# Hybrid mLSTM and attention step on one core: the output weights are gated and summed mid-kernel and kept in DRAM, the last stage leaves GpSimd, and the samples' rows lie as four column quarters

## The chip, the cores and the metric

The kernel runs on one core of one Trainium2 chip. A core has a matrix engine (TensorE, PE in the profile; its weight loads are shown apart as PEld), a vector engine (VectorE, DVE), an activation engine (ScalarE, ACT), a general engine (GpSimd, POOL) and SyncE (SP), which here only issues DMAs. The engines run side by side. Each works through its own instructions in program order, and they wait for one another by semaphores. Operands lie in SBUF (128 partitions), TensorE writes its results into banks of PSUM, and everything else lies in DRAM. In the code V, S and G stand for VectorE, ScalarE and GpSimd, `dma` for a DMA issued by SP and `mm` for a matmul.

The metric is the device time of one execution in microseconds (us), lower is better.

## The reference

One layer of a decoder is computed for 1024 prompt rows and 32 sample rows (8 sequences of 4), D = 1024, in float32:

```python
h, gate = adaln_in(x, c, w_ada, b_ada, g_norm)      # gate: one row of 1024 per sequence
(mq, mk, mv, mi, mf, mo, mz, aq, ak, av, az, gm, ga) = split_in(h @ w_in)
y_m, C, n, m = mlstm_branch(...)                     # 4 heads of 128
y_a = sliding-window attention with sinks(...)       # 8 heads of 64, window 128
u = sigmoid(gm) * (y_m @ w_mo) + sigmoid(ga) * (y_a @ w_ao)
x = x + gate * (u @ w_o)
y = rmsnorm(x, g_final)                              # rows of the prompt: y_p, of the samples: y_s
```

The mLSTM states, the kept keys and values and some smaller outputs are written as well. The last two lines matter here. All prompt rows share one gate row of 1024 values, so that `gate * (u @ w_o)` is the same as `u @ (w_o * gate)` with each column of `w_o` scaled by its gate value. The sample rows have gates of their own.

## The kernel before, in words

**Arithmetic.** TensorE multiplies in a short format (float32r in the code). A float32 operand is therefore split into a high half (a rounded copy, made by ScalarE) and a low half (the operand minus the high half, made by VectorE or GpSimd), and a product is three matmuls: high by high, high by low and low by high. Names ending in `h` and `l` (`u3whA`, `u3wlA`, `wo_t1l`) are such halves. Large products are cut into 2 by 2 blocks and formed from seven products of sums of blocks in place of eight products. The seven operands made of a weight's blocks are called `b11`, `b21`, `b22`, `t1` to `t4` here.

**Stages.** The layer norm and h (to about 66 us of the span), then the heads' projections, the attention and the mLSTM in jobs that a planner interleaves (to about 617 us), then `att_out` and `mem_out`, eight jobs each, which multiply by `w_ao` and `w_mo` and add up u (617 to 741 us), and the last stage, u @ w_o with the residual and the last norm (from 741 us).

**What sets the order.** Up to 617 us a planner (`side`, a list of generators on named streams) decides what comes next: each generator yields the modelled time until its next step may be placed, so the order on every engine comes from the planner's costs. `job` interleaves the outputs of one product with the loads and splits of the next. In the last stage the order is written out by hand: `V.on = S.on = G.on = True` keeps the instructions of each engine in the order of the program. SP issues all DMAs of this part from one queue in order, and its DMAs take turns on eight semaphores, so that a DMA cannot be issued before the one eight places ahead of it has landed.

**`mem_out`, before.** While the eight jobs run, SP loads the sixteen 128x512 pieces of `w_out`, VectorE forms the sums of blocks (`out_sums`), ScalarE and VectorE or GpSimd split the results into the high and low halves `wo_...h` and `wo_...l` that the last stage uses. For d above 5 the addition to u is on GpSimd.

**The last stage, before.** Four blocks of 256 rows (class `Rows`); each has the seven products, 6 matmuls each, and four plain products of 12 matmuls, 90 matmuls of 128x512 in all. The results lie in four PSUM banks `foX`, `foW`, `foY`, `foZ`; `copied` copies one bank to another (ScalarE), from where the next products are added to it. `Rows.start` makes the halves of a block's row operands (`u3whA` and `u3wlA` are those of block 3) while the block ahead of it runs. `add_part` multiplies a result by the gate (`gbc`) into `fot` and adds it to the residual rows in `rows_l`; `gated_ahead` does the same on GpSimd for the results `foy` and `fop`. `norm_rows` sums the squares and finds the reciprocal root by three Newton steps (`recip_sqrt`; names `fv`, `fr_w`, `fr_y`), and `rows_out` multiplies by it and by `g_final` (`gf`) and stores y_p.

**The sample rows.** `sample_rows` is a generator that the last stage advances at fixed places (`aside`). It multiplies the 32 sample rows of u by the unscaled `w_out`, which is loaded a second time: per half of 512 columns there are eight steps k, which go in turn to the four column groups of the array (32 columns each), so that four partial sums lie below one another in a bank `fo`; they are added by VectorE into `fo8s`, and GpSimd applies gate and residual.

Line numbers of the profile: L273 is the helper of all matmuls, L221 that of all VectorE, ScalarE and GpSimd operations, L260 that of SP's DMAs.

Of the kernel before, what the change touches and what calls it, by code (L numbers as in the profile page):

```python
# [174 lines left out]
def body(tc, a):  # L175
    nc = tc.nc
    with ExitStack() as ctx:
# [102 lines left out]
        def recip_sqrt(half, shape, name):  # L280
# [5 lines left out]
            for _ in range(3):  # L286
                if shape[1] == 1:
                    V.scalar_tensor_tensor(w, yi, half, yi, op0=ALU.mult, op1=ALU.mult)
                else:
                    V.tensor_tensor(w, yi, yi, op=ALU.mult)  # L290
                    V.tensor_tensor(w, w, half, op=ALU.mult)
                V.scalar_tensor_tensor(yi, w, 1.5, yi, op0=ALU.subtract, op1=ALU.mult)
# [755 lines left out]
        def head(h):  # L1048
# [100 lines left out]
            for visit in ([(load, 0), 10.0, ""], [(prep, 0), 3.0, "o"], [(stage_e, 0), (stage_a, 0), 5.0, "o"],  # L1149
# [5 lines left out]
                for fn, p in visit[:-2]:  # L1155
                    fn(p)
                yield visit[-2:]
# [7 lines left out]
        def sample_head(h):  # L1165
# [39 lines left out]
            yield 4.0, ""  # L1205
            V.tensor_tensor(et, et, S_[:NS], op=ALU.mult)
            for vf, vm, w in vms:
                S.copy(vm[0:32, :w], vf[:, :w])
            yield 2.5, ""
            for vf, vm, w in vms:  # L1210
                V.tensor_tensor(vm[32:64, :w], vf[:, :w], vm[0:32, :w].bitcast(F32), op=ALU.subtract)
# [35 lines left out]


# [104 lines left out]

        OPERANDS = {1: "b11", 2: "b21", 3: "b22", 4: "t4", 5: "t1", 6: "t2", 7: "t3"}
# [453 lines left out]
        ymx = [lambda k, c0, n, x=x: ymt[x][:, k, c0:c0 + n] for x in range(2)]  # L1808
        for d in range(KT):
# [3 lines left out]
        wo, plain, held = {n: [] for n in ("b11", "b21", "b22", "t1", "t2", "t3", "t4")}, {}, {}  # L1813

        def out_split(name, t, eng):
            wo[name].append(tuple(ht([128, 512], f"wo_{name}{x}", F32R) for x in "hl"))
            hi, lo = wo[name][-1]
            S.copy(hi, t)
            eng.tensor_tensor(lo, t, hi.bitcast(F32), op=ALU.subtract)

        def out_sums(k):

            (b11, b12), (b21, b22) = held.pop(k), held.pop(k + 2)
            out_split("b22", b22, G)
            V.tensor_tensor(b22, b22, b12, op=ALU.subtract)
            V.tensor_tensor(b12, b12, b11, op=ALU.subtract)
            out_split("t1", b12, G)
            V.tensor_tensor(b11, b11, b22, op=ALU.add)
            out_split("b21", b21, G)
            out_split("t3", b22, V)  # L1830
            V.tensor_tensor(b21, b21, b11, op=ALU.subtract)
            out_split("t2", b11, G)
            out_split("t4", b21, V)

        for d, k in enumerate((0, 2, 1, 3, 4, 5, 6, 7)):
            mem_out(d, ymx, u)
            raws = []
            for i in range(2):
                raws.append(raw_tile(f"wo{k}_{i}").rearrange("p k n -> p (k n)"))
                dma(raws[i], a["w_out"][k * 128:(k + 1) * 128, HALF[i]], True)  # L1840
            if k < 4:
                held[k] = raws
                if k < 2:
                    out_split("b11", raws[0], V)
                else:
                    out_sums(k - 2)
                continue
            for i, raw in enumerate(raws):
                plain[k, i] = (ht([128, 512], f"wo_h{k}", F32R), ht([128, 512], f"wo_l{k}", F32R) if (k, i) == (7, 1) else
                               granule(f"wo_l{k}", "wr", 9, F32R).rearrange("p k n -> p (k n)"))  # L1850
                S.copy(plain[k, i][0], raw)
                (G if i else V).tensor_tensor(plain[k, i][1], raw, plain[k, i][0].bitcast(F32), op=ALU.subtract)

# [4 lines left out]
        gbc, gsb, gf = misc[:3]  # L1858
        dma(gbc, gbD.to_broadcast((128, D)))
        dma(gf, a["g_final"].to_broadcast((128, D)))  # L1860
        dma(gsb[:NS], gsD)

        def residual(tb, n):
            xb = misc[3 + tb % 4 if tb < 8 else 7]
            dma(xb[:n], a["x_prompt"][tb * 128:tb * 128 + 128] if tb < 8 else a["x_sample"])
            return xb

        def add_part(xb, src, gb, n, cf, ss, mult=V, add=V):
            t = ht([128, 512], "fot")[:n, :cf.stop - cf.start]
            mult.tensor_tensor(t, src, gb[:n, cf], op=ALU.mult)  # L1870
            add.tensor_tensor(xb[:n, cf], xb[:n, cf], t, op=ALU.add)
            if ss is not None:
                square(xb[:n, cf], ss)

        def norm_rows(ss, m, parts):
# [6 lines left out]
            return recip_sqrt(v, [128, m], f"fr{m}")  # L1882

        def rows_out(tb, xb, r, by=V):
            yo, n = (a["y_p"][tb * 128:tb * 128 + 128], 128) if tb < 8 else (a["y_s"], NS)
            for c, eng in zip(HALF[::-1], (by, V if tb == 7 else by)):
                if eng is S:
                    S.activation(xb[:n, c], xb[:n, c], AF.Copy, scale=r[:n])
# [273 lines left out]
```

## Time and profile before

| | |
|---|---|
| time, three runs | 848.74, 850.94, 850.16 us (median 850.16) |
| profiled execution, its own time | 851.53 us |
| its span in the profile | 849.7 us |
| TensorE matmuls busy | 816.6 us (96%) |
| TensorE weight loads busy | 681.2 us (80%), under matmuls |
| VectorE busy | 614.9 us (72%) |
| ScalarE busy | 393.9 us (46%) |
| GpSimd busy | 172.9 us (20%) |
| read from DRAM, written | 110.78 MB, 41.61 MB |

All times in the views are counted from the start of the span, and the profiled execution took 1.83 us outside it. A busy share of 96% says that TensorE bounds the kernel as a whole; what is left are the stretches in which it waits, the stretches in which its clock is reduced, and what lies ahead of its first and behind its last matmul. A row of the timeline gives start, duration, engine, line, operation, output<-inputs and shape, and in square brackets the idle time before it with the instruction that ended it. Rows marked x2 or x4 hold several like instructions in a row. [...]

### The profile page before, as it was taken

The page shows a single profiled execution, that of the slowest core. Times are in us where ns is not written, and L with a number is a line of the kernel's source. Part 1 is how long each engine was busy: PE and PEld are TensorE (multiplying, and loading weights), DVE is VectorE, ACT ScalarE, POOL GpSimd, SP SyncE. Part 2 cuts the span into 40 slices and gives each one's busy share as a digit, 9 for nine tenths or more (in the row PEclk, how much of TensorE's full clock was granted, in tenths as well). Part 3 has the DMA queues.
Part 4 walks back from the last instruction along what each step waited for, and adds up shares of the span by engine and source line. Part 5 has one row for each costly group of instructions (what it writes and reads, how often), then busy time and mean ns, then how long its engine had stood idle before and what let it go on. Part 6 is the DMA issues. An engine that isn't in the chain of part 4 may idle for free. (4 is left out here: it accounts for less than half of the span.)

```text
span 849.7 us, 15293 instructions
## 1 busy us (share of the span) xinstructions
PE 816.6 (96%) x5083; PEld 681.2 (80%) x5083; DVE 614.9 (72%) x1634; ACT 393.9 (46%) x987; POOL 172.9 (20%) x236
## 2 busy tenths in 40 slices
PE   6899999999999899999999999999999999999984
PEld 3689988887899678778887777777788999967863
DVE  3787796666776867767667566888766679857987
ACT  4672356656654444455445344434443333223334
POOL 0220000330332335111211000000012033532563
PEclk9999999999999899999999999999999999999988
DMA  9996766775758866664534445553335974272322
GB/s 329 364 364 201 193 180 202 204 235 175 219 159 241 214 178 149 173 191 116 154 101 133 126 122 143 163 165 106 112 92 192 348 257 137 89 248 84 112 100 105
DMA packets 125330, 152.39 MB, mean 179 GB/s; under 512 B 28912, under 2 KB 79856, under 8 KB 125220
## 3 DMA queue, kind: packets, MB, share of 16 engines
q1 hardware_dynamic: 121028, 145.12, 55.1%
q0 software_dynamic: 4224, 6.30, 3.2%
q8 instruction: 40, 0.66, 0.3%
q14 instruction: 38, 0.31, 0.1%
HBM read 110.78 MB, written 41.61 MB: 179 GB/s over the span
## 5 line engine op out<-in xcount | busy, mean ns | idle before, releaser
L256 POOL DMA_DIRECT2D yhD<-yt x48 | 28.8, 606 | 114.3 <-DVE yt L221 108.0
L273 PE MATMUL g_w_ao<-ya,wh_w_ao 128*128 128x384 f32 (+1 forms) x192 | 45.7, 322 | 0.1
L273 PE MATMUL g_w_mo<-ym_l,wh_w_mo 128*128 128x384 f32 (+1 forms) x192 | 45.7, 323 | 0.0
L221 ACT ACTIVATE p<-p,nmx 128x256 f32<-128x256 f32 (+1 forms) x64 | 31.0, 486 | 23.2 <-DVE nmx L221 20.6
L256 POOL DMA_DIRECT2D mkN<-mkt x44 | 26.9, 618 | 50.6 <-DVE mkt L221 23.5
L273 PEld LDWEIGHTS g_w_ao<-ya,wh_w_ao 128*128 128x128 f32 x192 | 33.4, 188 | 0.7 <-DVE ya L221 0.6
L273 PEld LDWEIGHTS g_w_mo<-ym_l,wh_w_mo 128*128 128x128 f32 x192 | 33.5, 188 | 0.0
L273 PE MATMUL g_aq<-h_h,wh_aq 128*128 128x384 f32 (+1 forms) x96 | 32.5, 339 | 0.0
L256 POOL DMA_DIRECT2D mvN<-mvt x40 | 24.8, 625 | 35.5 <-DVE mvt L221 22.0
L221 DVE CUSTOM_DVE_ANT_0 p<-sc,cst,sink 128x256 f32<-128x256 f32 (+1 forms) x64 | 26.0, 461 | 7.5 <-PE sc L273 7.5
L273 PE MATMUL g_aq<-h_h,wl_aq 128*128 128x384 f32 (+1 forms) x96 | 31.0, 323 | 0.0
L273 PE MATMUL g_aq<-h_l,wh_aq 128*128 128x384 f32 (+1 forms) x96 | 31.0, 323 | 0.0
L273 PE MATMUL g_w_mo<-ym_l,wl_w_mo 128*128 128x384 f32 (+1 forms) x96 | 31.0, 323 | 0.0
L273 PE MATMUL g_w_ao<-ya,wl_w_ao 128*128 128x384 f32 (+1 forms) x96 | 30.8, 321 | 0.0
L273 PE MATMUL g_mq<-h_h,wh_mq 128*128 128x384 f32 (+1 forms) x72 | 24.9, 345 | 0.0
L273 PE MATMUL g_mk<-h_h,wh_mk 128*128 128x384 f32 (+1 forms) x72 | 24.5, 340 | 0.0
L273 PE MATMUL g_mk<-h_l,wh_mk 128*128 128x384 f32 (+1 forms) x72 | 23.3, 323 | 0.0
L273 PE MATMUL g_mq<-h_l,wh_mq 128*128 128x384 f32 (+1 forms) x72 | 23.2, 323 | 0.0
L273 PE MATMUL g_mk<-h_h,wl_mk 128*128 128x384 f32 (+1 forms) x72 | 23.2, 323 | 0.0
L221 POOL TENSOR_TENSOR ya<-yr,ya 128x384 fp32r<-128x384 f32 (+1 forms) x6 | 7.3, 1229 | 78.4 <-DVE hg L221 65.0
L273 PE MATMUL g_mq<-h_h,wl_mq 128*128 128x384 f32 (+1 forms) x72 | 23.2, 323 | 0.0
L221 POOL COPY qs<-mk 128x32 f32<-128x32 f32 x3 | 0.6, 212 | 104.6 <-ACT mk L221 104.6
(1702 smaller groups left out, 2803.0 us busy)
## 6 DMA issues: line engine op xcount, KB each, us to landing
hb<-hD SPq DMA_DIRECT2D x24, 256.0 KB
x<-xT SPq DMA_DIRECT2D x16, 256.0 KB
early_h<-w_ada SPq DMA_DIRECT2D x8, 512.0 KB
hD<-x SPq DMA_DIRECT2D x16, 256.0 KB
adar_ga<-w_ada SPq DMA_DIRECT2D x16, 256.0 KB
wr_ga<-w SPq DMA_DIRECT2D x16, 256.0 KB
wr_gm<-w SPq DMA_DIRECT2D x16, 256.0 KB
taD<-gt SPq DMA_DIRECT2D x16, 256.0 KB
```

The lines of the kernel that those rows point to most:

```text
L221: ins = f(*args, **kw)
L256: nc.gpsimd.dma_start(out, in_)
L273: in_order(nc.tensor.matmul(out, lhsT, rhs, start=start, stop=stop, skip_group_check=more))
```

## The change

1. **Scaled weights, mid-kernel.** A new generator `out_weights` is put on the planner's stream "x" in the stage of the last head. It loads the prompt's gate row (`ogb`) and `w_out` once, in four batches of four 128x512 pieces, multiplies them by the gate on VectorE (16 operations), forms the block sums there (8 operations), and stores the 14 operand tiles (`woD`) and the 8 plain tiles (`wpD`), 256 KB each, in DRAM.
2. **`att_out` and `mem_out`** load these 22 tiles (`out_load`) and split each one job later (`out_split`: high half on ScalarE, low half on VectorE). The sums and GpSimd's splits are gone from there, and all additions to u are on VectorE.
3. **The last stage** needs no multiplication by the gate: `add_part` is one addition on VectorE, and `gated_ahead` and `final_gain` are gone. GpSimd keeps only the Newton steps of the norm, 12 operations of 128x2 or 128x1 per pair of row blocks (the very last norm stays on VectorE); the squares are taken one by one, and one high half goes to y_p through ScalarE's DMA queue.
4. **The sample rows** lie as four quarters of 256 columns in four groups of 32 partitions: each step k has four matmuls of 256 columns, one for each column group, and no partial sums are left to add. The weights come 512 KB at a time, two tiles, in four loads. Residual, gate and `g_final` come by twelve small DMAs, and the sum of squares over the quarters by four small matmuls (`ft`).
5. In the sample heads of the middle, copies and splits of `vm` are spread over more planner steps.

```diff
-        def recip_sqrt(half, shape, name):
+        def recip_sqrt(half, shape, name, eng=V):
...
+                    eng.tensor_tensor(w, yi, yi, op=ALU.mult)
+                    eng.tensor_tensor(w, w, half, op=ALU.mult)
+                if eng is V:
+                    V.scalar_tensor_tensor(yi, w, 1.5, yi, op0=ALU.subtract, op1=ALU.mult)
+                else:
+                    eng.tensor_scalar(w, w, 1.5, None, op0=ALU.subtract)
+                    eng.tensor_tensor(yi, w, yi, op=ALU.mult)
...
+                if h == NH - 1 and visit[0] == (stage_b, 2):
+                    side.add("x", out_weights())
...
+        def out_weights():
+            gb = [ht([128, 512], f"ogb{i}") for i in range(2)]
...
+            def scaled(ks):
+                ts = []
+                for k in ks:
+                    for i in range(2):
+                        ts.append(ht([128, 512], f"ow{i}"))
+                        dma(ts[-1], a["w_out"][k * 128:(k + 1) * 128, HALF[i]])
+                yield 7.0, ""
+                for j, t in enumerate(ts):
+                    V.tensor_tensor(t, t, gb[j % 2], op=ALU.mult)
+                    if j % 2:
+                        yield 1.5, ""
+                return ts
+            for k in range(2):
+                b11, b12, b21, b22 = yield from scaled((k, k + 2))
+                for n, t in (("b11", b11), ("b22", b22), ("b21", b21)):
+                    store(woD[n][k], t)
+                yield 8.0, ""
+                V.tensor_tensor(b22, b22, b12, op=ALU.subtract)
+                V.tensor_tensor(b12, b12, b11, op=ALU.subtract)
+                yield 1.5, ""
...
+            for k in (4, 6):
+                ts = yield from scaled((k, k + 1))
+                for j, t in enumerate(ts):
+                    store(wpD[k - 4 + j // 2, j % 2], t)
+                yield 4.0, ""
...
-                (G if d > 5 else V).tensor_tensor(us, us, t, op=ALU.add)
+                V.tensor_tensor(us, us, t, op=ALU.add)
...
+        def out_split():
+            while coming:
+                hi, lo = coming.pop(0)
+                S.copy(hi, lo.bitcast(F32))
+                V.tensor_tensor(lo, lo.bitcast(F32), hi.bitcast(F32), op=ALU.subtract)
+        early, mid = dict(((4, 1), (5, 1), (6, 1), (7, 3))), (3, 3, 2, 2, 2, 2, 2, 0)
...
+        for d in range(KT):
             mem_out(d, ymx, u)
+            out_split()
+            out_load(mid[d])
...
-        def add_part(xb, src, gb, n, cf, ss, mult=V, add=V):
-            t = ht([128, 512], "fot")[:n, :cf.stop - cf.start]
-            mult.tensor_tensor(t, src, gb[:n, cf], op=ALU.mult)
-            add.tensor_tensor(xb[:n, cf], xb[:n, cf], t, op=ALU.add)
+        def add_part(xb, src, cf, ss=None):
+            V.tensor_tensor(xb[:, cf], src, xb[:, cf], op=ALU.add)
...
-        def norm_rows(ss, m, parts):
+        def norm_rows(ss, m, parts, eng=G):
...
+            load(0)
+            by_quarter(gs8, gsD)
+            by_quarter(x8, a["x_sample"])
+            by_quarter(gf8, a["g_final"].to_broadcast((NS, D)))
             yield
+            for k0 in (0, 2, 4, 6):
+                for k in (k0, k0 + 1):
+                    for j in range(4):
+                        mm(acc[32 * j:32 * j + 32], u(k, SEQ, NS), raws[k % 2][:, 256 * j:256 * j + 256],
+                           start=(k == 0), stop=(k == KT - 1), share=4)
+                if k0 < 6:
+                    load(k0 + 2)
                 yield
```

**How the order moves.** First VectorE in the last stage, between block 2 and block 3. Before, from the last use of `foZ` of block 2, with `u3wlB` and `u3wlC` the low halves for block 3:

```order
L221 TENSOR_TENSOR fot<-foZ,rows_l_8802 128x512
L221 SCALAR_TENSOR_TENSOR rows_l_8803<-rows_l_8803,fr_y,rows_l_8802 128x512 x4
L221 TENSOR_TENSOR u3wlB<-u_h_7748,u3whB 128x256
L221 TENSOR_TENSOR u_h_7748<-u_h_7748 128x2x128
L221 TENSOR_TENSOR u3wlB<-u_h_7748,u3whB 128x256
L221 TENSOR_TENSOR fot<-foW,rows_l_8802 128x512
L221 TENSOR_TENSOR rows_l_8802<-rows_l_8802,fot 128x512
L221 TENSOR_TENSOR u3wlC<-u_h_7749,u3whC 128x512
```

The same place in the changed kernel, with the rows ahead of it that lead up to it:

```order
L221 TENSOR_TENSOR u_h_7838<-u_h_7838 128x2x128 x2
L221 SCALAR_TENSOR_TENSOR rows_l_8875<-rows_l_8875,fr_y,rows_l_8874 128x512 x2
L221 TENSOR_TENSOR rows_l_8875<-foy_9413,rows_l_8875 128x512
L221 TENSOR_TENSOR rows_l_8875<-foZ,rows_l_8875 128x512
L221 SCALAR_TENSOR_TENSOR rows_l_8875<-rows_l_8875,fr_y,rows_l_8874 128x512 x2
L221 TENSOR_TENSOR u3wlB<-u_h_7838,u3whB 128x256
L221 TENSOR_TENSOR u_h_7838<-u_h_7838 128x2x128
L221 TENSOR_TENSOR u3wlB<-u_h_7838,u3whB 128x256
L221 TENSOR_TENSOR rows_l_8874<-foW,rows_l_8874 128x512
```

Two of the four row outputs have moved ahead of the work on `foy` and `foZ`, the multiplication into `fot` is gone, and the nine Newton operations that stood ahead of the first `fot` row before are no longer on this engine.

Next GpSimd in the last stage. Before, at the same place (`fop` and `foy` are results that wait for gate and residual, `fo8s` the sample sums):

```order
L221 TENSOR_TENSOR fop_9233<-fop_9233,rows_l_8802 128x512
L221 TENSOR_TENSOR rows_l_8802<-rows_l_8802,fop_9233 128x512
L221 TENSOR_TENSOR fot<-fo8s,rows_l_8802 32x512
L221 TENSOR_TENSOR rows_l_8803<-rows_l_8803,fot 32x512
L221 TENSOR_TENSOR foy_9325<-foy_9325,rows_l_8802 128x512
L221 TENSOR_TENSOR rows_l_8803<-rows_l_8803,foy_9325 128x512
L221 TENSOR_TENSOR rows_l_8803<-rows_l_8803,fot 128x512
```

In the changed kernel GpSimd's whole work there is made of such rows (the last three on the samples' rows, then the first on the next row block):

```order
L221 TENSOR_TENSOR fr_w<-fr_w,fv_9343 128x1
L221 TENSOR_SCALAR fr_w<-fr_w 128x1
L221 TENSOR_TENSOR fr_y<-fr_w,fr_y 128x1
L221 TENSOR_TENSOR fr_w<-fr_y 128x2
L221 TENSOR_TENSOR fr_w<-fr_w,fv 128x2
L221 TENSOR_SCALAR fr_w<-fr_w 128x2
L221 TENSOR_TENSOR fr_y<-fr_w,fr_y 128x2
```

All operations of 512 columns have left this engine, and the Newton steps have come to it from VectorE.

Last SP's queue in the middle of the kernel, where `wr_ga` and `wr_gm` are raw weights, `taD` and `tmD` stored gate halves, and `C_p` and `n_p` outputs. Before:

```order
L260 DMA wr_ga_1_5721<-w 128x512
L260 DMA C_p<-C 128x128
L260 DMA n_p<-C 128x1
L260 DMA taD_161<-gts 128x32
L260 DMA tmD_169<-gts 128x32
L260 DMA wr_gm_0_5723<-w 128x512
```

In the changed kernel, from the first store of a scaled tile:

```order
L260 DMA woD_b_157<-ow_5497 128x512
L260 DMA woD_b_158<-ow_5501 128x512
L260 DMA taD_169<-gt 128x512
L260 DMA C_p<-C 128x128
L260 DMA woD_b_159<-ow_5503 128x512
L260 DMA n_p<-C 128x1
L260 DMA wr_gm_0_5742<-w 128x512
L260 DMA wr_gm_1_5744<-w 128x512
```

The weights `wr_gm` of the next products stand behind three stores, each of which can be issued only when VectorE has scaled its tile.

More of the change, by code (lines that the diff above doesn't have):

```diff
@@ L1812, in body @@
                 split(ymD, *ymx, PCOLS, d // 2)
[L1813 to L1835, printed above, removed]
-            mem_out(d, ymx, u)
[L1837 to L1852, printed above, removed]
+            out_split()
+            out_load(early.get(d, 0))
+        for d in range(KT):
+            mem_out(d, ymx, u)
+            out_split()
+            out_load(mid[d])
+        assert not items and not coming
         assert not due
@@ new lines, in sample_rows @@
+            s8 = sm([128, 1], "fs8", 1)
+            square(x8, s8)
+            yield
+            tot = po([128, 1], "ft8")
+            for j in range(4):
+                mm(tot[32 * j:32 * j + 32], cst[:, C_S32:C_S32 + NS], s8, start=True, stop=True, share=4)
+            v8 = sm([128, 1], "fv8", 1)
+            V.tensor_scalar(v8, tot, 0.5 / D, 0.5 * EPS, op0=ALU.mult, op1=ALU.add)
+            r8 = recip_sqrt(v8, [128, 1], "fr1", G)
+            yield
+            V.scalar_tensor_tensor(x8, x8, r8, gf8, op0=ALU.mult, op1=ALU.mult)
@@ L1937, in body @@
+            for j in range(4):
+                dma(a["y_s"][:, 256 * j:256 * j + 256], x8[32 * j:32 * j + 32])
         class Rows:
```

177 lines of the change are left out of this document (86 added, 91 removed).

## The prediction

> **What bounds the kernel now.** I read the page first, then PE's waits in the last stage, a table of stretches, and the timelines at each wait. The page's busy shares:
>
> ```profile
> PE 816.6 (96%) x5083; PEld 681.2 (80%) x5083; DVE 614.9 (72%) x1634; ACT 393.9 (46%) x987; POOL 172.9 (20%) x236
> PEclk9999999999999899999999999999999999999988
> ```
>
> PE is busy nearly throughout, so only three things can be gained: waits of PE, a lowered clock (the digits 8 at the end of the second row), and what follows the last matmul. PE's waits from 740 us to its last matmul (total, times, longest):
>
> ```profile
> PE foX L273 <- ACT foW L221: 4.2, 2, 4.0
> PE fo L273 <- DMA rows_l<-w_out: 0.9, 1, 0.9
> ```
>
> The busy time of the engines by stretch (PE, PEld, DVE, ACT, POOL, granted clock, DMA share, GB/s):
>
> ```profile
> 430.00:450.00 20.00, 20.00 (x122) 16.32 (x121) 12.54 (x42) 8.05 (x19) 2.45 (x4) 1.00 0.44 120
> 540.00:560.00 20.00, 20.00 (x131) 16.07 (x131) 19.09 (x42) 10.08 (x22) 0.00 (x0) 1.00 0.52 161
> 700.00:720.00 20.00, 20.00 (x125) 20.00 (x124) 18.03 (x30) 5.38 (x10) 5.96 (x4) 1.00 0.45 136
> 786.00:810.00 24.00, 24.00 (x107) 19.84 (x107) 21.90 (x39) 8.93 (x23) 12.84 (x9) 1.00 0.32 99
> 810.00:838.00 28.00, 23.56 (x116) 19.71 (x114) 24.21 (x43) 12.70 (x32) 18.71 (x14) 0.88 0.32 113
> ```
>
> The middle and `mem_out` keep PE at 20.00 of 20, and the loss lies in the last 28 us, where the clock falls to 0.88. PE there:
>
> ```profile
> 812.13 0.39 PE L273 MATMUL foZ<-wo_t1l,u3whA 128*128 128x512 f32 x1
> 812.36 0.39 PE L273 MATMUL foZ<-wo_t1h,u3wlA 128*128 128x512 f32 x1
> 816.76 0.79 PE L273 MATMUL foX<-wo_b21h,u3whB 128*128 128x512 f32 x1 [4.02 <-ACT foW L221]
> 817.35 0.63 PE L273 MATMUL foX<-wo_b21l,u3whB 128*128 128x512 f32 x1
> 821.94 0.40 PE L273 MATMUL foX<-wo_h,u3whC 128*128 128x512 f32 x1
> ```
>
> In stream two starts lie 0.23 us apart (812.13 to 812.36; 0.2265 over longer runs). Between 812.36 and 821.94 lie thirteen steps, 2.94 us at that pace, and 9.58 went by: **6.64 us lost**, 4.17 as the wait and 2.47 as twelve slow steps of 0.43 behind it. The copy that PE waited for had itself waited for DVE:
>
> ```profile
> 816.14 0.57 ACT L221 COPY foW<-foX 128x512 f32<-128x512 f32 x1 [8.35 <-DVE fot L221]
> ```
>
> And DVE was late, because operations with two inputs in SBUF take longer beside POOL (DVE rows, then POOL's):
>
> ```profile
> 802.32 1.51 DVE L221 TENSOR_TENSOR u_h<-u_h 128x256 f32<-128x256 f32 x1
> 804.30 0.43 DVE L221 TENSOR_TENSOR u3wlA<-u_h,u3whA 128x256 fp32r<-128x256 f32 x1 [0.47 <-ACT u3whA L221]
> 806.42 1.25 DVE L221 TENSOR_SCALAR fv<-fss 128x2 f32<-128x2 f32 x1
> 809.95 0.69 DVE L221 TENSOR_TENSOR fot<-foZ,rows_l 128x512 f32<-128x512 f32 x1
> 810.56 3.76 DVE L221 SCALAR_TENSOR_TENSOR rows_l<-rows_l,fr_y,rows_l 128x512 f32<-128x512 f32 x4
> 815.37 0.68 DVE L221 TENSOR_TENSOR fot<-foW,rows_l 128x512 f32<-128x512 f32 x1
> ...
> 802.19 1.35 POOL L221 TENSOR_TENSOR rows_l<-rows_l,fot 32x512 f32<-32x512 f32 x1
> 806.29 1.35 POOL L221 TENSOR_TENSOR rows_l<-rows_l,foy 128x512 f32<-128x512 f32 x1
> ```
>
> The 128x256 operation at 802.32 took 1.51 us beside POOL, its like at 804.30 without it 0.43. `fv`, two columns wide, took 1.25 and ended at 807.67, POOL's operation at 807.64.
>
> **The change part by part.**
>
> *The stall.* Per row block DVE did nine Newton operations, four row outputs and six pairs of gate and add beside 12.84 us of POOL, 21.90 us of 24.00. Now for a block, by these rows: operand splits and sums 16 x about 0.42 (6.7), six additions at 0.69 (4.1), four row outputs at 0.75 (3.0), four small ones (0.7): an estimate of 14.5 us in a block of 90 x 0.2265 = 20.4 us. With 5.9 us to spare per block, the read of `foW` should no longer be late. Term **-6.64** (bounds: 0 if DVE still lags as much, -6.64).
>
> *The samples' wait.* Before and in a later group of eight:
>
> ```profile
> 752.84 1.06 PE L273 MATMUL fo<-rows_l,u_h 128*32 128x512 f32 x6
> 754.75 1.04 PE L273 MATMUL fo<-rows_l,u_h 128*32 128x512 f32 x2 [0.85 <-DMA rows_l<-w_out]
> 755.73 0.50 PE L273 MATMUL foZ<-wo_h,u0whD 128*128 128x512 f32 x1
> 777.58 1.06 PE L273 MATMUL fo<-rows_l,u_h 128*32 128x512 f32 x8
> 778.58 0.50 PE L273 MATMUL foZ<-wo_h,u1whD 128*128 128x512 f32 x1
> ```
>
> The first took 2.89 us, the later one 1.00. Its first products now stand at the end of block 0, some 15 us after the load can start: **-1.89**. The new groups have eight matmuls of 256 columns; I take 1.0 us each, as before (a group of half the columns can be no dearer by these rows; 0.5 each would be -2).
>
> *New waits there.* Two of the three later loads have 24 matmuls, 5.4 us, between their issue and their use. A load of 1 MB in the trace:
>
> ```profile
> 762.47 2.18 SPq L260 DMA_DIRECT2D rows_l<-w_out  x4
> 766.00:768.00 2.00, 2.00 (x11) 1.65 (x10) 1.16 (x2) 0.00 (x0) 0.00 (x0) 1.00 0.56 211
> 768.00:770.00 2.00, 2.00 (x10) 1.66 (x9) 1.90 (x4) 0.98 (x2) 0.00 (x0) 1.00 0.00 0
> ```
>
> From the first issue to empty DMA engines it is 4.6 us (by the share 0.56 of 766 to 768, about 767.1) to 5.5. Against 5.4 the wait is 0 to about 0.3, more where y_p stores or residual rows stand ahead in SP's queue. **+0.5** (0 to +2.5).
>
> *The start.* PE's second, short wait for `foW` (4.2 less 4.0, about 0.2 us) lay beside POOL's last additions to u: **-0.2** (0 to -0.7).
>
> *The tail.*
>
> ```profile
> 837.30 0.28 PE L273 MATMUL foY<-wo_h,u3wlD 128*128 128x256 f32 x1
> 835.49 1.21 DVE L221 SCALAR_TENSOR_TENSOR fr_y<-fr_w,fr_y 128x1 f32<-128x1 f32 x1
> 838.43 0.16 DVE L221 SCALAR_TENSOR_TENSOR fr_y<-fr_w,fr_y 128x1 f32<-128x1 f32 x1
> 844.95 0.75 DVE L221 SCALAR_TENSOR_TENSOR rows_l<-rows_l,fr_y,rows_l 128x512 f32<-128x512 f32 x1
> 834.15 1.29 POOL L221 TENSOR_TENSOR rows_l<-rows_l,foy 128x512 f32<-128x512 f32 x1
> 37.45 0.32 POOL L221 TENSOR_TENSOR h_l<-xS,h_h 128x64 fp32r<-128x64 f32 x1
> 36.25 0.82 POOL L221 TENSOR_TENSOR xS<-xS,B 128x64 f32<-128x64 f32 x1
> ```
>
> PE ends at 837.58, and the span 12.1 us later. Block 6's Newton steps, each held by a POOL operation, ended at 838.59, and DVE still had both remaining results to gate and add. Now POOL does these steps. They can start some 3.6 us ahead of PE's end (behind the last `foW`, its square and `fv`). Nothing of 128x1 is in the trace on POOL; the nearest are the two POOL rows of 128x64, 0.32 alone and 0.82 beside DVE. By 0.35 a step, twelve take 4.2 us and end 0.6 us after PE. Then come DVE's two row outputs (1.5), two additions (0.85), square and sums (0.75), its own Newton steps (1.7), the output (0.75) and the last store as before (4.0 from 845.7): 10.2 us after PE in place of 12.1. **-1.9** (-4 with steps of 0.2, +3.5 with 0.8, since DVE waits behind them in order). [...]
>
> *`ft`, extra small operations:* **+0.3**, four 32-column matmuls with their loads.
>
> *The middle:* 24 x 0.69 = 16.6 us more on DVE over about 110 us, where it is busy 12.5 to 14 of 20 us and 19.09 at 540, and 10 MB of DMA at a share of 0.44 to 0.52. What hides it is the lead of the splits over PE:
>
> ```profile
> 549.65 0.68 DVE L221 TENSOR_TENSOR wl_phead_gate__6690<-wr_mo,wh_phead_gate__6689 128x512 fp32r<-128x512 f32 x1
> 556.35 0.39 PE L273 MATMUL bx<-h_h,wl_phead_gate__6690 128*128 128x512 f32 x1
> ```
>
> This one, in the fullest stretch, is ready 6.0 us early. **0** (0 to +3). In `mem_out` DVE loses POOL's company and its sums and gains twelve splits and six additions, about 5.3 us per job of 7: **0**.
>
> Sum: -6.64 - 1.89 + 0.5 - 0.2 - 1.9 + 0.3 = -9.8, from 851.53 to 841.7. That execution lies 1.37 above the median of 850.16, so against the runs I expect **840.3 us**.
>
> **The rivals.**
>
> *A. DVE stays behind.* In a block DVE's row outputs wait in order for POOL's Newton chain, and behind them stand the next block's splits. As `fv` waited for POOL until 807.64, each of the twelve POOL steps may wait for a DVE operation of 0.42 to 0.75. Against it: once DVE stands still the chain runs free, so it holds DVE for at most 12 x 0.32 = 3.8 us per block, less than the 5.9 spare. If it happens all the same, or DVE's long operations weren't POOL's doing (the change then doesn't do what it says), I take half of the 6.64 to stay, in one stall of 3 to 4 us or several short ones: 840.3 + 3.3 = 843.6, up to 847 with all of it. [...]
>
> *B. The gain is eaten.* The stall goes, but POOL's chain at the end takes 0.8 a step (+5.4 against my sum) and each of three sample loads costs 1 us (+2.5): 848.2, no change. For it: no POOL operation so small is in the trace, and the 128x64 rows vary from 0.32 to 0.82. Against it: DVE has little to do while the last chain runs.
>
> *C. Slower: the middle.* SP issues in order, and stores of `woD` stand ahead of `wr_gm`. Each can be issued only when DVE has scaled its tile, and that waits for its load. If this holds SP or DVE longer than the 6.0 us lead, PE waits. A wait that lowers the clock costs 6.64, as at 812; two such would give 840.3 + 13.3 = 853.6, and slower begins from 12.4 us of waits. For C: DVE's 19.09 of 20. Against: in the stretch at 430, where the first batch falls, DVE is idle 7.5 of 20 us. [...]
>
> **How the numbers follow.** Chances: the forecast 0.58, A 0.22, B 0.09, C 0.11. The forecast's own range is 836 (tail -4, groups at 0.5 us) to 843; the whole range runs to 848, through A and up to B, and leaves out C, half of B and the best luck. What cannot be told from no change is 0.3%, 2.5 us: above 847.6 to 852.7. Forecast, A and a third of B give faster 0.83; the rest of B and a mild C give 0.08 the same; C in full gives 0.09 slower.
>
> **What would show it.** Right: no idle PE of more than 1 us behind 741 us, a granted clock of 1.00 from 810 to PE's end, DVE's 128x256 operations at 0.42 throughout, DVE's busy time near 15 us per row block. The last matmul comes some 8 us earlier, and 10 us lie behind it. Wrong: a wait of `fo8` for `w_out` above 1 us, POOL rows `fr_w` above 0.5 us with DVE idle before the row outputs, or PE idle between 430 and 740 us behind `wl_` or `wr_` tiles.

## The result and the profile after

The changed kernel takes 841.83 us (median of four runs, 840.93 to 842.38), the kernel before 849.45 us beside it: a ratio of 0.9907 (95% interval 0.9889 to 0.9926), 7.6 us less. The forecast was 840.3 us in a range of 836 to 848, so the direction and the range held, and the gain was 7.6 to 8.3 us (by the two medians of before) where 9.8 were worked out. The profiled execution took 842.23 us with a span of 840.4, to be set against 851.53 and 849.7.

The page of the changed kernel, shares of busy time and granted clock:

```profile
PE 812.5 (97%) x5123; PEld 680.3 (81%) x5123; DVE 596.4 (71%) x1636; ACT 387.4 (46%) x975; POOL 117.0 (14%) x245
PEclk9999999999999999999999999999999999999998
HBM read 116.55 MB, written 47.37 MB: 195 GB/s over the span
```

The lowered clock of the last fortieths is gone but for the tail, and 11.5 MB more are moved. PE's waits from 420 us to the end are a single row, and not behind the `wl_` or `wr_` tiles that the prediction named:

```profile
PE sU L273 <- DVE Cs L221: 1.3, 1, 1.3
```

The last stage by row block (columns as before), and PE's first and last matmul in it:

```profile
741.00:761.00 20.00, 20.00 (x105) 16.11 (x105) 9.86 (x22) 6.32 (x16) 0.00 (x0) 1.00 0.59 204
761.00:784.00 23.00, 23.00 (x131) 17.22 (x133) 11.51 (x25) 7.43 (x19) 2.71 (x12) 1.00 0.51 173
784.00:808.00 24.00, 24.00 (x121) 19.27 (x114) 15.62 (x37) 9.98 (x27) 6.50 (x24) 1.00 0.29 102
808.00:830.70 22.70, 22.63 (x123) 19.51 (x121) 10.98 (x25) 7.18 (x20) 5.26 (x24) 1.00 0.27 94
...
742.42 0.40 PE L273 MATMUL foX<-wo_h,u0whA 128*128 128x512 f32 x1
830.35 0.28 PE L273 MATMUL foY<-wo_h,u3wlD 128*128 128x256 f32 x1
```

PE is never idle there, the clock is 1.00 throughout, and DVE, which had 21.90 of 24.00 and 24.21 of 28.00 us before, has 10 to 15.6. Block 2's place, where DVE was late, now reads:

```profile
805.93 0.43 DVE L221 TENSOR_TENSOR u3wlB<-u_h,u3whB 128x256 fp32r<-128x256 f32 x1
806.39 0.43 DVE L221 TENSOR_TENSOR u_h<-u_h 128x256 f32<-128x256 f32 x1
807.07 0.68 DVE L221 TENSOR_TENSOR rows_l<-foW,rows_l 128x512 f32<-128x512 f32 x1
```

**Time by part.** With the last stage from its first matmul's start to its last one's end, and the tail from there to the end of the span, the two profiles divide like this (us):

| | before | after | difference |
|---|---|---|---|
| span up to the last stage | 740.83 | 742.42 | +1.59 |
| last stage | 96.75 | 88.21 | -8.54 |
| tail | 12.12 | 9.77 | -2.35 |
| span | 849.70 | 840.40 | -9.30 |

The same table for every kernel run here. The first column is the one that scatters: it goes from 738.98 to 746.77 over seven profiles whose code is the same up to the last stage (the changed kernel twice, e1, e5, e6, e8 and e6 with another tail order).

| kernel | to last stage | last stage | tail | median time |
|---|---|---|---|---|
| changed | 742.42 | 88.21 | 9.77 | 841.83 |
| changed, again | 738.98 | 88.21 | 9.81 | 841.17 |
| e1 GpSimd busy | 740.90 | 91.67 | 10.53 | 845.10 |
| e5 last norm on VectorE | 741.08 | 88.21 | 9.71 | 841.22 |
| e6 all norms on VectorE | 741.06 | 88.21 | 9.13 | 840.14 |
| e7 later scaling | 739.60 | 88.22 | 9.88 | 840.81 |
| e8 waits | 739.58 | 89.84 | 9.78 | 842.51 |
| e9 no scaling operations | 737.17 | 88.21 | 10.12 | 838.70 |
| e6 with another tail order | 746.77 | 88.21 | 8.22 | 840.98 |
| before, e2 less gate | 741.66 | 92.84 | 10.60 | 845.29 |
| before, e3 GpSimd silent | 739.39 | 89.44 | 8.07 | 838.17 |
| before, e4 no sample sums | 740.42 | 91.15 | 14.93 | 847.80 |
| before, e10 all on VectorE | 738.97 | 92.14 | 13.59 | 847.41 |

### The profile page after: what moved, and what is told of

Its sections match the earlier page's. It is cut to its first block, busy times and chain, and to the rows that moved or that the text cites. A ratio compares the mean times of both kernels' runs of the same rounds, so it can differ in the third digit from the quotient of the medians.

```text
span 840.4 us, 15436 instructions
## 1 busy us (share of the span) xinstructions
PE 812.5 (97%) x5123; PEld 680.3 (81%) x5123; DVE 596.4 (71%) x1636; ACT 387.4 (46%) x975; POOL 117.0 (14%) x245
## 5 line engine op out<-in xcount | busy, mean ns | idle before, releaser
L221 POOL TENSOR_TENSOR fr_w<-fr_y 128x2 f32<-128x2 f32 (+1 forms) x15 | 3.1, 208 | 159.5 <-DVE fr_y L221 139.3
L221 ACT ACTIVATE gt<-gt 128x512 f32<-128x512 f32 (+1 forms) x17 | 10.4, 613 | 25.3 <-DVE gt L221 24.7
```

The lines of the kernel that those rows point to most:

```text
L221: ins = f(*args, **kw)
```

## The experiments

The theory from the prediction (A) was that the stall of 4.02 us and the slow steps behind it came from VectorE being held up by GpSimd on top of its own load. The first rivals are that GpSimd's company alone, the gate's multiplications alone, or the samples' work in block 2 made it.

**e1: company without the work.** Nine additions on GpSimd are put into each row block:

```diff
+        def pool_busy(n):
+            for _ in range(n):
+                G.tensor_tensor(idle[1], idle[0], idle[0], op=ALU.add)
...
             add_part(xb[0], p5, hi)
+            pool_busy(3)
```

> The changed kernel with nine useless additions of 128x512 on GpSimd put back into each row block of the last stage (11 to 12 us per block, about what GpSimd did there before; nothing waits for their results). Theory A: the stall came from the lengthening of VectorE's operations beside GpSimd together with VectorE's own load, and both had to go; VectorE now needs 10 to 13 us of the 20 to 22 per block, and company adds 4 to 7, so it stays below the block's time: 128x256 operations at 0.8 to 1.5 us in place of 0.42, but PE waits under 1 us in the stage and the time rises by 0 to 2 us (842 to 844). Theory B: GpSimd's company alone makes the stall: a wait of 3 us or more of foX for ACT's copy is back with slow steps behind it, +5 to +7 us (847 to 849).

Measured: 845.1 us (ratio 0.9951, 0.9929 to 0.9973). The wait for `foW` did not come back; three smaller ones came, and the stage grew by 3.46 us:

```profile
PE ft L273 <- ACT sq L221: 1.2, 1, 1.2
PE foY L273 <- ACT foy L221: 1.1, 1, 1.1
PE foZ L273 <- DVE u0wlD L221: 0.6, 1, 0.6
```

So B is out, and A's figures (waits under 1 us, 0 to 2 us) were too low: with VectorE at 16.7 of 22 us in block 2 there is still slack on average, and PE waits all the same, since single chains (the samples' sum, the copy of `foy`) have none. Company cost 3.46 us of the stage here, where it did not fill VectorE.

**e2: the kernel before without VectorE's gate multiplications** (for `foX`, `foW`, `foY`):

```diff
-            mult.tensor_tensor(t, src, gb[:n, cf], op=ALU.mult)
-            add.tensor_tensor(xb[:n, cf], xb[:n, cf], t, op=ALU.add)
+            if mult is V and add is V:
+                V.tensor_tensor(xb[:n, cf], src, xb[:n, cf], op=ALU.add)
```

> The kernel before, with the gate's multiplication left out where VectorE did both the multiplication and the addition (the results foX, foW and foY are added ungated, so the output differs); GpSimd's work is as before. VectorE loses three operations of 0.69 us per row block. Theory A (load and company together, with samples' work in block 2): only about 0.7 to 1.4 us of what is lost stands in the 16 us of full VectorE work ahead of the late read of foW, so a wait of 2 to 3.5 us stays, and the time falls by 1 to 2.5 us (847 to 848.5). Theory C (the multiplications were the cause): the wait is gone, -6 to -7 us (843).

Measured: 845.29 us (0.9947, 0.9930 to 0.9963).

```profile
816.03 0.50 PE L273 MATMUL foX<-wo_b21h,u3whB 128*128 128x512 f32 x1 [2.24 <-ACT foW L221]
816.37 0.39 PE L273 MATMUL foX<-wo_b21l,u3whB 128*128 128x512 f32 x1
816.60 0.40 PE L273 MATMUL foX<-wo_b21h,u3wlB 128*128 128x512 f32 x1
```

The wait is 2.24 us, inside A's 2 to 3.5, and C is out. But the time fell by 4.3 us in place of 1 to 2.5: no slow steps follow the shorter wait (starts 0.23 us apart). The stage is 3.91 us shorter, as 1.8 us less of waiting took the 2.5 of slow steps with it, and the tail 1.52, which A had not counted. The last section shows that waits of about this length are followed by slow steps in some executions and not in others, so the 2.5 need not be won in each.

**e3: the kernel before with GpSimd silent** in the last stage:

```diff
-            G.tensor_tensor(t, t, gbc[:, c], op=ALU.mult)
-            G.tensor_tensor(xb[:, c], xb[:, c], t, op=ALU.add)
+            pass
```

and likewise for the final gain, the samples' gate and residual, and the addition of `foZ`.

> The kernel before, with all of GpSimd's operations of the last stage left out (its gates, residual additions and final gain, so the output differs); VectorE does what it did. Theory A: VectorE's 128x256 operations take 0.42 throughout, its small operations 0.17, the four seconds it lacked ahead of foW are there, the stall and its slow steps vanish (-6.6 us) and the tail is shorter by 2 to 3 us since its Newton steps are no longer held: 839.5 to 841.5. Theory C: VectorE's operations keep their lengths, and the stall stays within 1 us.

Measured: 838.17 us (0.9873, 0.9849 to 0.9898). PE's waits and VectorE's groups in block 2:

```profile
PE fo L273 <- DMA rows_l<-w_out: 0.2, 1, 0.2
PE foX L273 <- ACT foW L221: 0.2, 1, 0.2
...
L221 DVE SCALAR_TENSOR_TENSOR rows_l<-rows_l,fr_y,rows_l 128x512 f32<-128x512 f32 x3 | 2.2, 744 | 0.0
L221 DVE TENSOR_TENSOR u_h<-u_h 128x256 f32<-128x256 f32 x4 | 1.7, 422 | 0.1
```

VectorE still multiplies by the gate, adds the samples and takes its Newton steps. An operation on `u_h` takes 422 ns on average; the one at 802.32 took 1.51 us before. With GpSimd silent the stall is gone, and the tail is 4.05 us shorter, more than expected, which puts the time below A's range. VectorE could also have been late by waiting for results of GpSimd, but the rows exclude that: from `fot<-foX` of block 2 to `fot<-foW` it takes 16.06 us before (799.31 to 815.37) and 10.52 here (797.14 to 807.66), and its one wait for another engine in between is 0.47 us for ScalarE in both. The difference is in the length of its operations. This settles that GpSimd's operations made VectorE late.

**e4: the kernel before without the samples' sums**, six operations on VectorE and four on GpSimd:

```diff
-                for j in (32, 64, 96):
-                    V.tensor_tensor(sums[f], acc[f][j:j + 32], sums[f], op=ALU.add)
...
-            for f in range(2):
-                add_part(xb, sums[f], gsb, NS, HALF[f], None, G, G)
```

> The kernel before, with the adding up of the samples' partial sums on VectorE (six operations of 0.69) and their gate and residual on GpSimd (four operations of 32x512, 1.35 to 1.7 each) left out, so y_s is wrong. Rival D: the samples' work in block 2 was the drop too much: VectorE gains 2.1 us of its own and about 3 us of lengthening there, against a wait of 4.0: wait under 0.5 us, no slow steps, -5.5 to -6.6 us (843 to 844). Theory A without D: the stall would need the load of all the blocks, and 2 us or more of the wait stays.

Measured: 847.80 us (0.9981, 0.9968 to 0.9995). The wait shrank to 1.35 us without slow steps, between the two expectations, and the stage by 5.60 us. But the time fell only by 1.8: the tail grew from 12.12 to 14.93. The rows say why (VectorE, then GpSimd):

```profile
824.41 1.21 DVE L221 SCALAR_TENSOR_TENSOR fv<-fss,fv 128x3 f32<-128x3 f32 x1
829.07 1.21 DVE L221 SCALAR_TENSOR_TENSOR fr_y<-fr_w,fr_y 128x3 f32<-128x3 f32 x1
836.77 0.42 DVE L221 TENSOR_TENSOR fot<-foY,rows_l 128x256 f32<-128x256 f32 x1
...
819.75 5.85 POOL L221 TENSOR_TENSOR rows_l<-rows_l,rows_l 128x512 f32<-128x512 f32 x4
833.09 1.27 POOL L221 TENSOR_TENSOR rows_l<-rows_l,rows_l 128x512 f32<-128x512 f32 x1 [2.83 <-ACT sq L221]
837.74 1.26 POOL L221 TENSOR_TENSOR rows_l<-rows_l,rows_l 128x512 f32<-128x512 f32 x1 [3.37 <-ACT sq L221]
```

PE ended at 831.57, and VectorE read its last results 5.2 us later, because its small operations took up to 1.21 us, as at 835.49 before (0.16 at 838.43). The gain in the stage came off PE's end and was given back behind it. Relieving PE alone was worth little; the tail's own GpSimd work had to go too.

**e10: was the amount of work the matter?** All of GpSimd's operations of the stage go to VectorE in the kernel before (`G` becomes `V` in the places of e3):

> The kernel before, with all of GpSimd's operations of the last stage given to VectorE, the gate's multiplications kept: nothing in the middle is changed and nothing is stored in DRAM. VectorE needs 15 to 16 us per row block without GpSimd's company (measured with those operations left out), and gets 3.5 more, in block 2 another 2.8: 19 to 22 of about 22. Theory A (the company was the cause, not the amount of work): a wait of foX for foW of at most 1.5 us, no slow steps, the last matmul 5 to 7 us earlier in its stage, and 841 to 845 us. Rival B (the gate's work had to leave the stage): the wait of 3 us or more is back, and the time is within 2 us of 849.6.

Measured: 847.41 us (0.9972, 0.9952 to 0.9993).

```profile
PE foZ L273 <- DVE u0wlD L221: 1.3, 1, 1.3
PE foZ L273 <- DVE u2wlD L221: 0.8, 1, 0.8
PE foX L273 <- ACT foW L221: 0.4, 2, 0.2
```

The wait for `foW` stays away, as A has it, but neither A nor B came out whole, as the time lies between them: splits are late instead, and the tail is 13.59 us, as the additions and gains stand in one queue. So GpSimd's company had to go, and the work could not simply be moved to VectorE. That gating the weights ahead of time is what lets VectorE take the rest is argued and not shown apart: no run has the gating without the new layout of the samples' rows and the new order.

**The tail.** In the changed kernel VectorE waited for GpSimd's Newton steps from 829.08 to 830.86, across PE's end at 830.63:

```profile
828.43 0.70 POOL L221 TENSOR_TENSOR fr_w<-fr_w,fv 128x1 f32<-128x1 f32 x1
830.63 0.19 POOL L221 TENSOR_TENSOR fr_y<-fr_w,fr_y 128x1 f32<-128x1 f32 x1
828.38 0.69 DVE L221 TENSOR_TENSOR rows_l<-rows_l,rows_l 128x512 f32<-128x512 f32 x1 [0.84 <-ACT sq L221]
830.86 1.41 DVE L221 SCALAR_TENSOR_TENSOR rows_l<-rows_l,fr_y,rows_l 128x512 f32<-128x512 f32 x2 [1.78 <-POOL fr_y L221]
832.19 0.74 DVE L221 TENSOR_TENSOR rows_l<-foY,rows_l 128x256 f32<-128x256 f32 x2
```

e5 is `rs = norm_rows(ss, 1, 2, V)` in the last block:

> The changed kernel with the Newton steps of row block 6 (the norm ahead of the last one) on VectorE in place of GpSimd. In the changed kernel VectorE waited 1.78 us for GpSimd's last step behind PE's end. Theory A (order on VectorE decides): the steps take 1.4 us of VectorE ahead of the addition of foZ, and the square of that row, the gain and the two row outputs still follow one another, so that the last row is only 0.2 to 0.6 us earlier (841.3 to 841.7). Rival B: the whole wait of 1.78 us goes: 840.0.

Measured: 841.22 us (0.9906, 0.9891 to 0.9920). The last additions end 1.78 us behind PE in place of 2.30, 0.52 earlier and inside A's 0.2 to 0.6, though 1.78 us of waiting for GpSimd went: the addition of `foZ`, its square and the gain still stand one behind another. The end of the span came only 0.06 us earlier behind PE (tail 9.71 against 9.77), as the last output was followed by 4.45 us in place of 3.96. (The expectation for the last version gives 1.64 in place of the 1.78 of these rows.)

e6 has all norms on VectorE, the samples' too:

> The changed kernel with all Newton steps on VectorE, none on GpSimd. Theory A (VectorE has 7 to 10 us to spare per row block once gate and samples are gone): 1.8 us more per block do not reach PE, no wait in the stage, the same time as with the last norm alone moved (841 to 842). Rival B (moving the steps off VectorE was needed): waits of foX or of a split of 1 us or more return in blocks 2 or 3, +1 to +4 us.

Measured: 840.14 us (0.9889, 0.9870 to 0.9908), no wait of PE in the stage, 88.21 us as before. Moving the Newton steps to GpSimd bought nothing for PE, and B is out.

The last version keeps e6 and changes the order in the tail:

```diff
                 add_part(xb[1], Z, hi, ss[:, 2:3])
-                V.tensor_tensor(xb[1][:, hi], xb[1][:, hi], gf[:, hi], op=ALU.mult)
                 rows_out(6, xb[0], rs)
...
                     add_part(xb[1], y, slice(c0, c0 + n), ss[:, f + 3:f + 4])
+                V.tensor_tensor(xb[1][:, hi], xb[1][:, hi], gf[:, hi], op=ALU.mult)
```

> The changed kernel with all Newton steps on VectorE, and in the last row block the two row outputs ahead of, and the multiplication of the last half row by the gain behind, the additions of foY. Theory A (VectorE's order decides the tail): the last additions end 0.4 to 0.6 us behind PE in place of 1.64 with the steps on VectorE alone and 2.30 in the changed kernel, so about 7.9 to 8.2 us lie behind PE's last matmul in place of 9.8, and the time is 1.2 to 2 us below the changed kernel's (839.8 to 840.6). Rival B (the squares on ScalarE or the last stores set the end): less than 0.7 us is gained.

> The changed kernel once more, beside the three others on the same chip: 841.8 within 1 us, a wait of PE for VectorE's sample update near 475 us of 0.5 to 2.2 us, no wait of PE in the last stage, and 9.5 to 10 us behind its last matmul.

Measured side by side: 840.98 (0.9892, 0.9866 to 0.9920) and 841.17 (0.9893, 0.9866 to 0.9920).

```profile
833.16 1.41 DVE L221 SCALAR_TENSOR_TENSOR rows_l<-rows_l,fr_y,rows_l 128x512 f32<-128x512 f32 x2
834.48 0.97 DVE L221 TENSOR_TENSOR rows_l<-foY,rows_l 128x256 f32<-128x256 f32 x2
835.36 0.68 DVE L221 TENSOR_TENSOR rows_l<-rows_l,rows_l 128x512 f32<-128x512 f32 x1
```

The profile does what A said: the last additions end at 835.45, 0.47 us behind PE (834.98), and the tail is 8.22 us in place of 9.81. The medians do not show these 1.6 us: the six times range from 838.29 to 844.96, and the longest is the profiled one, whose last stage began at 746.77. So the shorter tail is shown, and that the whole is faster than the changed kernel (840.98 against 841.17) is not.

**The middle.** PE's one wait there, with the rows around it: before, the bank `sU` was read by VectorE at 474.77 (0.56 of the 1.03 us) and needed by PE 1.5 us later.

```profile
474.77 1.03 DVE L221 TENSOR_TENSOR Cs<-Cs,sU 128x387 f32<-128x387 f32 x2 [0.25 <-PE sU L273]
476.82 0.28 PE L273 MATMUL sU<-vm,skn 96*128 96x258 f32 x1
```

After, four multiplications of `out_weights` stand ahead in VectorE's queue from 468.10 on, with waits of 0.67 and 2.04 us for their loads:

```profile
470.83 0.69 DVE L221 TENSOR_TENSOR ow<-ow,ogb 128x512 f32<-128x512 f32 x1 [2.04 <-DMA ow<-w_out]
477.05 1.02 DVE L221 TENSOR_TENSOR Cs<-Cs,sU 128x387 f32<-128x387 f32 x2
477.65 0.39 PE L273 MATMUL sU<-vm,skn 96*128 96x258 f32 x1 [1.34 <-DVE Cs L221]
```

e7 lets the planner wait longer (`yield 12.0` for `yield 7.0` behind the loads):

> The changed kernel with the planner told to leave 12.0 instead of 7.0 us between the loads of w_out in the middle and their multiplication. In the changed kernel VectorE waited four times for these loads (5.5 us in all), and PE once, 1.34 us at 477.65, for VectorE's sample update that stood behind. Theory A: VectorE's waits for ow fall below 1 us in all, PE's wait goes, and the time falls by 1.0 to 1.5 us (840.5). Rival B: it was VectorE's added 16.6 us of work as such; the wait stays or turns up elsewhere, same time within 0.5 us.

Measured: 840.81 us (0.9899, 0.9882 to 0.9917). VectorE's waits for `ow` were 4.9 us in all, so A's means did not work, and a new wait of 2.95 us for `wr_gm` stood near 468. PE's wait was 0.54 us, the lower end of what the same middle gave in other kernels. Nothing follows from it.

e9 leaves out the 24 operations and keeps all DMAs:

> The changed kernel with the 16 multiplications and 8 block sums of out_weights left out; its loads and stores, and so all DMA traffic, stay, and the stored tiles are raw pieces of w_out, so y_p differs. In the profiles of five kernels with this middle PE waited 0.54 to 2.17 us (mean 1.4) near 475 us for VectorE's sample update. Theory A (VectorE's added work and its waits for the loads make this wait): no wait of PE there, last stage starts 0.5 to 1.5 us earlier than in the other kernels with this middle (739 to 741), and the time falls by about 1 us. Rival B (the DMA traffic delays the weights of the products): a wait of PE of 0.5 us or more for a split or for ACT stays between 430 and 560 us.

Measured: 838.70 us (0.9866, 0.9836 to 0.9896). PE has no wait between 420 us and the end. The wait was 0.5 to 2.2 us in the seven other profiles with this middle. That the last stage begins at 737.17, the earliest of all, shows little by itself, since this number scatters; but the scatter lies ahead of 424 us. Counted from the third pair of matmuls `n<-hv,et` there, which stands ahead of the loads of `out_weights` (from 432.69 on), the way to the last stage can be compared (before, then e9, then the changed kernel):

```profile
424.64 0.39 PE L273 MATMUL n<-hv,et 128*128 128x129 f32 x2
740.83 0.40 PE L273 MATMUL foX<-wo_b11h,u0whA 128*128 128x512 f32 x1
...
421.05 0.39 PE L273 MATMUL n<-hv,et 128*128 128x129 f32 x2
737.17 0.40 PE L273 MATMUL foX<-wo_h,u0whA 128*128 128x512 f32 x1
...
424.73 0.39 PE L273 MATMUL n<-hv,et 128*128 128x129 f32 x2
```

It is 316.19 us before and 316.17 to 316.20 in e2, e3, e4 and e10, which have the same middle; 317.69 in the changed kernel (to its 742.42); 316.92 to 318.56 in its second run, e1, e5, e7, e8 and the last version, and 319.99 in e6, where slow steps follow the wait; and 316.12 in e9. So VectorE's added operations, with their waits for the loads, which e9 has not either, cost 0.7 to 2.4 us here (3.8 with slow steps), and the DMA traffic nothing that these numbers show. How much is the operations and how much their waits is not separated.

**e8: what a wait of PE costs.** Five and nine useless copies on ScalarE ahead of the copy to `foW`, in blocks 2 and 3:

> The changed kernel with useless copies on ScalarE ahead of the copy of foX to foW, five in row block 2 and nine in row block 3, so that PE is kept waiting about 2.0 and about 4.1 us in a stage that has no waits. Theory A (the clock is lowered only after a wait of some length, as the 4.02 us wait was followed by twelve steps of 0.43 and the 0.85 us wait by none): the first costs its 2 us alone, the second 4.1 and 1.5 to 2.7 of slow steps: +8 to +9 us (850). Rival B: both lower the clock: +10.5 to +11.5. Rival C: the slow steps had another cause: +6.

Measured: 842.51 us (0.9925, 0.9900 to 0.9950). The copies made waits of 0 and 1.33 us only, and no slow steps followed. The waits were not long enough to tell the theories apart; what other runs show is told below.

## Why the prediction was right

**What bounds the kernel.** Right: stall, slow steps, samples' wait and tail were where the gain lay. PE's idle time behind 741 us went from 5.1 us to none.

**The stall, -6.64, and the samples' wait, -1.89.** Right in size: together 8.53, the stage fell by 8.54. The reason given held (e3), with two corrections: VectorE needed 10 to 13 us a block and not 14.5 (9.86 of 20 to 15.62 of 24 us in the stretches), and the 2.47 us of slow steps do not belong to every wait (none in e2 and e4): by the last section they come where some 2 us of a wait fall into one interval of the clock's grid, which a wait of 4.02 us hardly escapes.

**New waits, +0.5, `ft`, +0.3, the start, -0.2.** None of the samples' loads was late, and the four groups took 1.00 us each, as taken. The three terms come to about 0 in place of +0.6.

**The tail, -1.9.** It measured -2.35. GpSimd's small operations take 0.19 to 0.23 us at a pitch of 0.28, against the 0.35 chosen from rows of 64 columns. One step, at 828.43, took 0.70 us beside VectorE's operation at 828.38. The rest of the chain was as worked out (rows out, additions, squares, Newton steps, 4.0 us of store).

**The middle, 0.** This is the step that failed: the term put at nothing. It measured +1.59 in this pair of profiles, 1.50 of it behind 424 us, where five profiles with the old middle agree to 0.03 us, and 1.34 of that is PE's wait for `sU`. The cover named was the 6.0 us lead of the weight splits, and the splits were indeed not late. But VectorE also empties PSUM banks for the sample heads, in the same queue, with 1.5 us of lead in the row at 474.77, and the prediction left that kind of operation out. This is the mechanism of rival C in small: a load awaited on VectorE, the queue behind it late, PE waiting.

**The offset.** The sum gave 841.7 us for a profiled execution, and that took 842.23. That it came so near is partly luck: the 1.59 us of the middle were offset by 0.45 in the tail and the 0.6 of the small terms. From there to the forecast 1.37 us were taken off, since the profiled execution before lay so far above the median; the changed kernel's lay 0.40 above its own, so 1.0 us of the miss of 1.5 is this.

**The rivals.** A (VectorE stays behind): some of GpSimd's steps were longer (four in a row of 0.38 to 0.59 us from 801.5 on, beside VectorE's row outputs and the addition of `foy`; 0.19 to 0.23 for most others), and VectorE had time for it. B: no sample load was late. C took its small form.

**A short wait and the clock.** The prediction took the lowered clock from one case, the wait of 4.02 us. A wait of 2.09 us in e6 was followed by slow steps of 0.42 to 0.44 us too, as the last section shows.

## What to carry to other kernels

Look at the engine that shares work with the busy one as a source of length, not only of help: work moved to GpSimd lengthened VectorE's operations by more than it took off them (VectorE is busy for 75.86 us of the last stage before and for 73.27 in e10, where it does GpSimd's work as well), and the cure was to make the work disappear from the stage (scale the weights once, ahead) rather than to move it back. When a term is set to zero because work is hidden, list every kind of operation in that engine's queue that another engine waits for, the emptying of PSUM banks too, and take the shortest lead, not the most frequent one. A gain at PE's end is worth only what the tail behind it does not take back, so compare stage and tail apart, and also the stretch around the change, above all where the run-to-run spread lies elsewhere.

## What the runs showed of the hardware

**The same short wait lowers the clock in one run and not in the next; where it falls decides.** Every profile here has the same wait of 2.81 us near 280 us, in code that no kernel changes. Two stretches behind it (granted clock is the third number from the right), in the kernel before and in the changed one:

```profile
281.00:283.00 2.00, 1.73 (x8) 1.73 (x9) 1.74 (x6) 0.00 (x0) 2.00 (x5) 0.50 0.51 109
...
281.00:283.00 2.00, 1.76 (x12) 1.63 (x13) 1.90 (x6) 0.56 (x2) 2.00 (x5) 1.00 0.79 183
```

In ten of fourteen profiles the clock was lowered during it or just behind it, for 3.41 or 6.83 us, in four (the changed kernel, e2, e3, e4) not at all. PE's wait for `sU` shows the same: 2.09 us in e6 was followed by slow steps, 2.18 us in e5 by none:

```profile
474.73 0.58 PE L273 MATMUL sU<-vm,skn 96*128 96x258 f32 x1 [2.09 <-DVE Cs L221]
475.10 0.63 PE L273 MATMUL bz<-h_h,wh_pgate__5895 128*128 128x512 f32 x1
...
476.31 0.39 PE L273 MATMUL sU<-vm,skn 96*128 96x258 f32 x1 [2.18 <-DVE Cs L221]
476.54 0.40 PE L273 MATMUL bz<-h_h,wh_pgate__5895 128*128 128x512 f32 x1
```

Waits up to 1.9 us with no other near them had no slow steps, those of 2 to 2.8 us sometimes, 3.18 us (in e4, at 344 us) none, and 4.02 us did.

Very short stretches of the same view show when the clock changes. In the kernel before:

```profile
279.00:279.08 0.08, 0.00 (x0) 0.00 (x0) 0.08 (x1) 0.08 (x1) 0.08 (x1) 1.00 0.89 288
279.09:279.17 0.08, 0.00 (x0) 0.00 (x0) 0.08 (x1) 0.08 (x1) 0.08 (x1) 0.50 0.88 288
...
814.88:814.96 0.08, 0.00 (x0) 0.00 (x0) 0.08 (x1) 0.00 (x0) 0.00 (x0) 1.00 1.10 410
814.98:815.06 0.08, 0.00 (x0) 0.00 (x0) 0.08 (x2) 0.00 (x0) 0.00 (x0) 0.50 0.91 333
```

These two falls lie 535.89 us apart, 157 times 3.4133, and both low stretches last 6.83 us, twice that. In each of the fourteen profiles all changes of the clock lie whole multiples of 3.413 us apart (to 0.01 us in the kernel before and the changed one), and the place of this grid differs from profile to profile. Call what lies between two points of the grid an interval, and count PE's idle time in each from 100 us on: of the intervals at full clock, the clock fell at the end of every one with 2.05 us or more (27 intervals, those behind the last matmul included), and of none with 1.82 us or less. The wait of 2.81 us in the changed kernel was divided by the end of an interval, at 279.42, into 0.99 and 1.82 us; in the kernel before, the interval that ended at 279.08 held 0.62 of it and 1.74 of another wait, 2.37 in all. The wait of 2.09 us in e6 lay in one interval, which ended at 474.73; the one of 2.18 us in e5 was divided into 0.67 and 1.51, that of 2.24 in e2 into 1.58 and 0.66, and that of 3.18 in e4 into 1.67 and 1.51. So by these numbers a wait of up to 1.8 us alone costs itself, one above 4.1 us, twice 2.05, lowers the clock wherever it falls, and in between its place decides; that is an estimate from the two bounds. Idle time is not all that counts: in the changed kernel the clock fell once ahead of the last matmul, at 67.80, behind an interval without idle time, in which 18 matmuls of 8 columns and 16 of 32 ran.

**A stage can be steady to 0.01 us while the kernel scatters.** The last stage took 88.21 or 88.22 us in seven profiles of kernels whose stage has no wait, while its start lay between 737.17 and 746.77. The stretch from 424 us to that start is as steady, 316.17 to 316.20 us in the five kernels with the middle of before. Differences of under 1% in a late stage are read there, and not in six times of the whole.
